# A third pair of split-weight buffers and a two-tile split lead in two windows of a diffusion backbone layer

## The chip, the core and the metric

One core of a Trainium2 chip runs the whole layer in one launch. The metric is device time in microseconds (us), lower is better. The kernel before takes 1840.38 us, the median of three runs (1839.56 to 1844.32).

## What is computed

The layer mixes 512 latent tokens of width 1024, on a grid 64 wide, with a prefix of 256 context tokens. The part that matters here, cut from the reference:

```python
hx = modulate(x, norm1_g, shift1, scale1);  hc = modulate(ctx, ...)
u_x, k_x, v_x, q_x, ga_x, gb_x = jnp.split(hx @ w_in, ...)     # 512 latent rows
u_c, k_c, v_c = jnp.split(hc @ w_in[:, :CTX_COLS], ...)        # 256 context rows
y_ssm = s5_mixer(u_x, u_c, p)               # bidirectional linear state recurrence
branch_a = s5_glu(y_ssm, p) @ w_branch_a
branch_b = na_mixer(q_x, k_x, v_x, k_c, v_c, na_rpb) @ w_branch_b
merged = sigmoid(ga_x) * branch_a + sigmoid(gb_x) * branch_b
x = x + gate1 * (merged @ w_out)
x = x + gate2 * peer_ffn(modulate(x, norm2_g, shift2, scale2), ...)
return rms_norm(x, final_g)
```

`s5_mixer` runs a scan over chunks of tokens; `peer_ffn` scores every token against all keys and experts. All is float32, and the projections are accurate beyond one reduced-precision pass.

## The kernel before

**Weight tiles.** A projection of 128 output columns is a tile of 1024 x 128 weights (some tiles have 512 rows). All tiles stand in one list, `wseq`, and are taken from it in order by `w_next` (L191): tiles 0 to 3 give u, 4 to 7 k, 8 to 11 v, 12 to 15 q, 16 to 51 are those of the two branches, the gates and the GLU, and from tile 52 on come the queries and experts of the feed-forward part. A tile is loaded by a DMA issued on SP into `wraw` (L183), rounded on ACT into `whi` (L172), and the remainder `wlo = wraw - whi` is taken on DVE (L173). TensorE then runs three passes for each of the 8 row blocks (`mm3`, L443 to L445): hi by x-hi, hi by x-lo, lo by x-hi. u, k and v tiles are also run over the context (output `mc`, against `mm` for the latent tokens).

**Buffers.** The pool `wst` has three `wraw` buffers and two each of `whi` and `wlo`. With tile i, `w_next` sees that tiles up to i+2 are loaded and that tile i+1 is split:

```python
w_ahead(i + 1, i + 1, eng)
wpos[2] += 1
w_ahead(i + 3, i + 2, eng)      # load below i+3, split below i+2
```

**Stages around the change** (times of the trace in us). Up to about 136 the outer products (`g_outer`, DVE, tile `Gc`), the kernel pieces (`k_prep`, L510 to L528: matmuls into `kk` and `yy`, a copy to `ks` on ACT at L522, stores `Kd<-ks` on SP at L526 to L528) and the first projections run together. `Gc`, `ks` and others lie in a pool `gst2` (L488), closed behind them. Then DVE sweeps the state `E` (`carry`, L610 to L613): sixteen passes of a tree, each pass two products `ta`, `tb_` and two additions into `E`; the products lie in the pool `scp` (L586). PE meanwhile projects k, v and q (L443 to L445 and, for v, transposes at L637). ACT copies the swept state to `S` (L641, L642). Attention follows from 222 to 310, one matmul chain of scores (L708, L709), softmax (DVE L710 and L712, ACT L714), transposes (L721) and values (L739), with the readout of the state. From about 310 to 460 PE runs the GLU, the branches and the gates, while DVE forms modulation vectors from streamed rows (`mod2`, L814), the gated sums (L829, L849) and the splits. Then come `wo_mm` with W_out, `x1_norm` (L922 to L931, with small tiles `ss`, `ry`, `rz` of two buffers each) and the feed-forward part.

**Order.** But for SP's first part, the order of instructions on each engine is set by a scheduler from the order of the calls; an engine then runs its list strictly in that order, and a waiting instruction holds up all behind it.

Of the kernel before, what the change touches and what calls it, by code (L numbers as in the profile page):

```python
# [10 lines left out]
F32 = mybir.dt.float32  # L11
F32R = mybir.dt.float32r
# [11 lines left out]
KD = 8  # L24
# [60 lines left out]
def tile_hybrid(ctx, tc, A, out, dbg=None):  # L85
# [3 lines left out]
    def open_pool(**kw):  # L89
        cm = tc.tile_pool(reuse_waits="tile", **kw)  # L90
        return cm, cm.__enter__()

    def close_pool(*cms):
        for cm in cms:
            cm.__exit__(None, None, None)

    def DBG(name, ap):
        if dbg is not None and name in dbg:
            sy.dma_start(dbg[name], ap)
# [9 lines left out]
    def bank(tag="mm", bufs=None):  # L109
        bufs = bufs or nb[tag]  # L110
        return (psA if tag in ("kk", "yy") else ps).tile([128, 512], F32, tag=tag, name=tag, bufs=bufs)
# [19 lines left out]
    wst = ctx.enter_context(tc.tile_pool(name="wst", bufs=1))  # L131
# [10 lines left out]
    def sm(name, *shape):  # L142
        return stp.tile([128, *shape], F32, name=name)

    wseq = [("win", m, KD) for m in range(16)]
    wkind = {"b": ("win", 24, KD), "a": ("win", 16, KD), "B": ("wb", 0, 4), "A": ("wa", 0, 4), "g": ("wglu", 0, 4)}
    for i, o in enumerate(MERGE):
        src, m0, kn = wkind[o]
# [2 lines left out]
    wseq += [("puT", j, KD) for j in range(UA)]  # L151
    wseq += [("wq", i, KD) for i in range(2 * NH)]
    wseq += [("puT", j, KD) for j in range(UA, 128)]
    mark = [None]
    wraw, wsp = {}, {}
    wext = {}
    wcnt = {}

    def wtile(kind, dt):
        n, x = wbufs[kind]  # L160
        c = wcnt[kind] = wcnt.get(kind, -1) + 1
        if wext and c % (n + x) >= n:
            return wext[0].tile([128, KD, 128], dt, tag=kind, name=kind, bufs=x)
        return wst.tile([128, KD, 128], dt, tag=kind, name=kind, bufs=n)
# [1 line left out]
    wbufs = {"wraw": (3, 2), "whi": (2, 1), "wlo": (2, 1)}  # L166
    wpos = [0, 0, 0]

    def w_split(raw, kn, eng):
        hi = wtile("whi", F32R)  # L170
        lo = wtile("wlo", F32R)
        act.copy(hi[:, :kn], raw[:, :kn])  # L172
        i = eng.tensor_sub(lo[:, :kn], raw[:, :kn], hi[:, :kn].bitcast(F32))  # L173
        if eng is gp:
            mark[0] = i.ins
        return hi, lo

    def w_ahead(load_to, split_to, eng):
        while wpos[0] < min(load_to, len(wseq)):
            i = wpos[0]  # L180
            src, m, kn = wseq[i]
            w = wtile("wraw", F32)
            sy.dma_start(w[:, :kn].rearrange("p k c -> p (k c)"), A[src][m])  # L183
            wraw[i] = w
            wpos[0] += 1
        while wpos[1] < min(split_to, len(wseq)):
            i = wpos[1]
            wsp[i] = w_split(wraw.pop(i), wseq[i][2], eng)
            wpos[1] += 1

    def w_next(want, eng=gp):  # L191
        i = wpos[2]
        assert wseq[i][:2] == want, (wseq[i], want)
        w_ahead(i + 1, i + 1, eng)
        wpos[2] += 1
        w_ahead(i + 3, i + 2, eng)
        return wsp.pop(i)

    order = tc.manual_schedule(engines={mybir.EngineType.SP})
# [15 lines left out]
    def rsqrt_mean(ss, y, z):  # L215
        dve.tensor_scalar(ss, ss, 1.0 / D, EPS, op0=ALU.mult, op1=ALU.add)
        dve.tensor_scalar(z.bitcast(I32), ss.bitcast(I32), 1, None, op0=ALU.logical_shift_right)
        dve.tensor_scalar(y.bitcast(I32), z.bitcast(I32), -1.0, 1597463007.0, op0=ALU.mult, op1=ALU.add)
        dve.tensor_scalar(ss, ss, -0.5, None, op0=ALU.mult)
        for _ in range(3):  # L220
            if y.shape[-1] == 1:
                dve.tensor_scalar(z, y, y, ss, op0=ALU.mult, op1=ALU.mult)
            else:
                dve.tensor_mul(z, y, y)
                dve.tensor_mul(z, z, ss)
            dve.scalar_tensor_tensor(y, z, 1.5, y, op0=ALU.add, op1=ALU.mult)
# [20 lines left out]
    for o in LDO:  # L247
        if o == "w":
            mod_rows(nw)
            nw += 1  # L250
        elif o == "s":
            sy.dma_start(ssm, A["ssm"][:, 0:1120])
        elif o == "p":
            sy.dma_start(colp, A["colp"])
        elif o == "r":
            sy.dma_start(crt.rearrange("p j g h -> p (j g h)"), A["ssm"][:, 1120:2144])
        elif o == "1":
            w_ahead(wpos[0] + 1, 0, gp)
        elif o == "x":
            x_t.append(load_x(A["x"], len(x_t)))  # L260
        else:
            c_t.append(load_x(A["ctx"], len(c_t)))
# [26 lines left out]
    dt, er, th = sm("dt", G), sm("er", G), sm("th", G)  # L289
# [46 lines left out]
    n = 1  # L336
# [114 lines left out]
    def project(m, ctx_too, eng=None):  # L451
        eng = eng or (dve, gp)[PJE(m)]
        w = w_next(("win", m), eng)
        a = bank()
        mm3(a, w, hxh, hxl, KD)
        if not ctx_too:
            return a, None
        c = bank("mc", 1)
        mm3(c[:, :CTXL], w, hch, hcl, KD)
        return a, c[:, :CTXL]  # L460

    w0 = w_next(("win", 0))
    wpos[2] += 1
    w1 = wsp.pop(1)
# [19 lines left out]
    ecm, ep = open_pool(name="ep", bufs=1, side="right")  # L484
# [89 lines left out]
    for o in SEQ1:  # L574
        m = nxt[o]
        nxt[o] += 1
        if o == "u":
            a, c = (a1, c1) if m == 1 else project(m, True)
# [4 lines left out]

    kcm, kp_ = open_pool(name="kp", bufs=1)

    sccm, scp = open_pool(name="scp", bufs=1, side="right")  # L586
    lam = [L8]
    for l in range(4):
# [40 lines left out]
    for m in range(4):  # L629
        a, c = project(8 + m, True)  # L630
# [3 lines left out]
        for j0, n in ((0, 4), (4, 3)):  # L634
            p = bank("tp")
# [10 lines left out]
    for m in range(4):  # L646
        a, _ = project(12 + m, False)
        av = a.rearrange("p (r j c) -> p r j c", r=8, c=16)
        for e in range(2):
            s, z = slice(64 * e, 64 * e + 64), slice(64 * (1 - e), 64 * (1 - e) + 64)  # L650
            gp.memset(qT[2 * m + e][z], 0.0)
            act.activation(qT[2 * m + e][s].rearrange("p (j r c) -> p r j c", r=8, c=16), av[s], AF.Copy, scale=0.125)
    close_pool(sccm, ecm)

    ycm, yp = open_pool(name="yp", bufs=1, side="right")
    Y = yp.tile([128, TC, SSMW // 2], F32, name="Y")
# [132 lines left out]
    for i in range(4):  # L789
        p = bank("tp")  # L790
# [8 lines left out]
        dve.tensor_sub(zl[i], zf[i], zh[i].bitcast(F32))  # L799
    DBG("zf0", zf[0])  # L800
    close_pool(ycm, xscm)

    mgcm, mgp = open_pool(name="mgp", bufs=1, side="right")
    mgh = [mgp.tile([128, SEQ], F32R, name=f"mgh{i}") for i in range(8)]
# [19 lines left out]
    def branch(which, m):  # L824
        w = w_next(("w" + which, m), dve)
        a = bank()
        xs = (ah, al) if which == "a" else (oh, ol)
        mm3(a, w, *xs, 4)
        dve.scalar_tensor_tensor(sgt[which, m], sgt[which, m], 1.0, a, op0=ALU.add, op1=ALU.mult)  # L829
# [70 lines left out]
    x1cm, x1p = open_pool(name="x1p", bufs=1)  # L900
# [22 lines left out]
    def x1_norm(t):  # L923
        sy.dma_start(x1d[t], x1[t])
        if t == 0:
            DBG("x1_0", x1[0])
        ss, y, z = (x1p.tile([128, 1], F32, tag=n, name=n, bufs=2) for n in ("ss", "ry", "rz"))
        jk = m2p.tile([128, D], BF16, tag="jk2", name="jk3", bufs=1)
        act.activation(jk, x1[t], AF.Square, accum_out=ss)
        rsqrt_mean(ss, y, z)  # L930
        act.activation(x1[t], x1[t], AF.Copy, scale=y)  # L931
# [25 lines left out]
    def wo_pass(ps_):  # L957
        for i in range(2):
            t = ps_ // 2 * 2 + i
            wo_out(ps_ % 2, t, wo_mm(ps_, t))  # L960
            if ps_ < 3:
                for k in range(4):
                    wo_load(ps_ + 1, 4 * i + k)
            if ps_ % 2:
                x1_norm(t)
# [8 lines left out]
    for half in range(2):  # L974
        p = bank("tp")
# [3 lines left out]
    DBG("hrow", hrow)  # L979
    close_pool(x1cm)  # L980
    close_pool(wocm, m2cm, mgcm)
    ugp = ctx.enter_context(tc.tile_pool(name="ugp", bufs=1))
    gate = ugp.tile([128, NT, 128], F32, name="gate")
    ijt = ugp.tile([128, 2, ND, 128], F32, name="ijt")
# [416 lines left out]
```

## Time and profile before

| | |
|---|---|
| runs (three) | 1839.56, 1840.38, 1844.32 us |
| profiled execution | 1838.56 us, of which the span of the trace is 1836.7 us |
| TensorE matmul busy | 1719.5 us (94% of the span) |
| VectorE (DVE) busy | 1471.2 us (80%) |
| ScalarE (ACT) busy | 779.4 us (42%) |
| GpSimd (POOL) busy | 354.0 us (19%) |
| mean granted TensorE clock | 0.973 |

Busy shares are means over stages that have different limits. So the windows of the changed stages are read one by one, and there the question is which engine's wait ends last. The granted clock is a share of TensorE's full clock.

### The profile page before, as it was taken

To read this page: it belongs to the slowest core of one execution; us is meant where nothing else is said; L and a number is where in the kernel's file an instruction comes from. 1 tells how busy PE (TensorE), PEld (TensorE's weight loads), DVE (VectorE), ACT (ScalarE), POOL (GpSimd) and SP (SyncE) were. 2 spreads that over 40 slices of the span, in tenths; PEclk is the share of its full clock that TensorE was granted. 3 is DMA by queue.
4 is the path that set the end of the run, shared out by engine and by line. 5 is a ranking of instruction groups with operands and counts; after the bars stand their busy time and mean duration, and the time that the engine had idled before them with its cause. 6 is when DMAs were issued, how large, how long until landed. Compare 5 with 4: busy or idle time off the path is not lost.

```text
span 1836.7 us, 27460 instructions
## 1 busy us (share of the span) xinstructions
PE 1719.5 (94%) x9941; PEld 1504.7 (82%) x9941; DVE 1471.2 (80%) x3054; ACT 779.4 (42%) x1214; POOL 354.0 (19%) x291
## 2 busy tenths in 40 slices
PE   5999899999999899995589999999999999999997
PEld 2878677778899799994579899999999999998885
DVE  8889765875699998999888788888878888884456
ACT  6452555432464346666333333333333333333332
POOL 0001000000000000000332444544545444440000
PEclk9999899999999999997699999999999999999999
DMA  8341362885544336765799899999999999994432
GB/s 334 95 134 59 95 165 58 286 292 166 201 140 140 116 117 189 207 196 170 223 406 356 273 345 348 329 342 352 318 339 359 336 327 344 341 336 128 127 119 75
DMA packets 186327, 426.15 MB, mean 232 GB/s; under 512 B 25552, under 2 KB 91216, under 8 KB 186192
## 3 DMA queue, kind: packets, MB, share of 16 engines
q1 hardware_dynamic: 84816, 231.44, 37.3%
q0 software_dynamic: 36864, 134.23, 20.2%
q10 hardware_dynamic: 64512, 58.73, 10.1%
q8 instruction: 78, 1.28, 0.3%
q14 instruction: 57, 0.47, 0.1%
HBM read 388.72 MB, written 35.62 MB: 231 GB/s over the span
## 4 chain that ended last, share of the span: by engine, by line
PE 73%; DVE 16%; DMA 5%; issue 2%; ACT 2%; SPq 0%; ACTq 0%; POOL 0%; DVEq 0%
PE acc L1273 10%; PE acc L1274 10%; PE acc L1275 10%; PE yy L445 5%; PE yy L443 5%; PE yy L444 5%; PE kk L445 5%; PE kk L443 5%; PE kk L444 5%; DVE wlo L173 3%; DMA wm<-in_wmodT_dram 3%; PE mm L443 2%; PE mm L445 2%; PE mm L444 2%; DMA Gt_d<-gs 1%
## 5 line engine op out<-in xcount | busy, mean ns | idle before, releaser
L172 ACT CAST whi<-wraw 128x1024 fp32r<-128x1024 f32 (+1 forms) x212 | 213.9, 1009 | 219.3 <-PE mm L444 100.3
L1156 POOL DMA_INDIRECT gu<-in_pu_dram,idx x128 | 167.6, 1309 | 590.1 <-ACT gs L1142 386.0
L173 DVE TENSOR_TENSOR wlo<-wraw,whi 128x1024 fp32r<-128x1024 f32 (+1 forms) x212 | 247.2, 1167 | 38.3 <-ACT whi L172 37.2
L1156 POOL DMA_INDIRECT gu<-in_pv_dram,idx x128 | 177.6, 1388 | 195.2 <-DVE gacc L1174 167.2
L1255 DVE TENSOR_TENSOR wlo<-wraw,whi 128x1024 fp32r<-128x1024 f32 x128 | 156.5, 1223 | 38.0 <-ACT whi L1254 37.7
L1163 DVE SCALAR_TENSOR_TENSOR gj<-gu,hrow 128x1024 bf16<-128x1024 f32 x128 | 156.1, 1220 | 29.6 <-DMA gu<-in_pu_dram,idx 29.2
L443 PE MATMUL yy<-hth,whi 128*128 128x384 f32 x512 | 174.7, 341 | 4.2 <-ACT whi L172 4.0
L1174 DVE SCALAR_TENSOR_TENSOR gacc<-gu,av,gacc 128x1024 f32<-128x1024 f32 x127 | 162.6, 1280 | 19.4 <-DMA gu<-in_pv_dram,idx 18.9
L445 PE MATMUL yy<-hth,wlo 128*128 128x384 f32 x512 | 174.7, 341 | 1.2 <-DVE wlo L173 1.2
L445 PE MATMUL kk<-hth,wlo 128*128 128x384 f32 x512 | 173.9, 340 | 1.4 <-DVE wlo L173 1.3
L443 PE MATMUL kk<-hth,whi 128*128 128x384 f32 x512 | 172.9, 338 | 2.4 <-ACT ring L954 2.4
L444 PE MATMUL yy<-htl,whi 128*128 128x384 f32 x512 | 174.0, 340 | 0.0
L444 PE MATMUL kk<-htl,whi 128*128 128x384 f32 x512 | 172.9, 338 | 0.0
L1254 ACT CAST whi<-wraw 128x1024 fp32r<-128x1024 f32 x128 | 133.7, 1046 | 67.7 <-PE kk L444 26.7
L1142 ACT ACTIVATE gs<-mm 128x512 f32<-128x512 f32 x96 | 94.1, 1090 | 56.1 <-PE mm L1140 53.4
L445 PE MATMUL mm<-hxh,wlo 128*128 128x512 f32 x256 | 103.8, 406 | 12.4 <-DVE wlo L173 12.4
L443 PE MATMUL mm<-hxh,whi 128*128 128x512 f32 x256 | 102.0, 403 | 4.7 <-ACT whi L172 3.0
L443 PEld LDWEIGHTS yy<-hth,whi 128*128 128x128 f32 x512 | 97.6, 191 | 7.5 <-ACT whi L172 4.7
L444 PE MATMUL mm<-hxl,whi 128*128 128x512 f32 x256 | 102.8, 402 | 0.0
L443 PEld LDWEIGHTS kk<-hth,whi 128*128 128x128 f32 x512 | 96.8, 189 | 4.5 <-ACT ring L954 2.7
L445 PEld LDWEIGHTS yy<-hth,wlo 128*128 128x128 f32 x512 | 97.3, 190 | 3.1 <-DVE wlo L173 1.7
L444 PEld LDWEIGHTS yy<-htl,whi 128*128 128x128 f32 x512 | 97.6, 191 | 2.3
(1911 smaller groups left out, 4217.4 us busy)
## 6 DMA issues: line engine op xcount, KB each, us to landing
wraw<-in_puT_dram SPq DMA_DIRECT2D x128, 512.0 KB
wraw<-in_pv_dram SPq DMA_DIRECT2D x128, 512.0 KB
Gt_d<-gs ACTq DMA_DIRECT2D x24, 1024.0 KB
gch<-Gt_d ACTq DMA_DIRECT2D x32, 768.0 KB
wraw<-in_win_dram SPq DMA_DIRECT2D x32, 512.0 KB
wm<-in_wmodT_dram SPq DMA_DIRECT2D x32, 512.0 KB
wraw<-in_wq_dram SPq DMA_DIRECT2D x32, 512.0 KB
wm<-in_wm_dram SPq DMA_DIRECT2D x16, 512.0 KB
```

The lines of the kernel that those rows point to most:

```text
L172: act.copy(hi[:, :kn], raw[:, :kn])
L173: i = eng.tensor_sub(lo[:, :kn], raw[:, :kn], hi[:, :kn].bitcast(F32))
L443: pe.matmul(o, hi[:, k], xh, start=(k == 0), stop=False)
L444: pe.matmul(o, hi[:, k], xl, start=False, stop=False)
L445: pe.matmul(o, lo[:, k], xh, start=False, stop=(k == kn - 1))
L1156: gp.indirect_dma_start(out=u, out_offset=None, in_=A[tab], in_offset=bass.IndirectOffsetOnAxis(ap=ix[:, s:s + 1], axis=0))
L1163: dve.scalar_tensor_tensor(jk, u, 1.0, hrow, op0=ALU.mult, op1=ALU.mult, accum_out=av[:, s:s + 1])
L1174: dve.scalar_tensor_tensor(gacc, u, av[:, s:s + 1], gacc, op0=ALU.mult, op1=ALU.add)
L1255: dve.tensor_sub(lo, w, hi.bitcast(F32))
L1273: pe.matmul(acc[t][half], wh_[:, ts], hi[:, cs], start=(j == 0), stop=False)
L1274: pe.matmul(acc[t][half], wh_[:, ts], lo[:, cs], start=False, stop=False)
L1275: return pe.matmul(acc[t][half], wl_[:, ts], hi[:, cs], start=False, stop=(j == 127))
```

## The change

A pool `wx` with one further `whi` and one further `wlo` buffer is opened twice, on the right side of the SBUF: from before the state sweep until q is projected, and from the GLU and branches until `wo_mm`, `x1_norm` and their pools are done. While it is open, every third tile of the string takes the `wx` pair, and loading and splitting run one tile further ahead (load below i+4, split below i+3), as far as tile 15 in the first window and tile 51 in the second. `ry` and `rz` in `x1_norm` go from two buffers to one. Line numbers after the change are higher by 6 up to L183, by 7 from there to `scp`, and by 9 to 12 behind it.

```diff
-    def wtile(kind, dt):
+    nwx = 0
+    wxp = None
+    def wtile(kind, dt, early=False):
         n, x = wbufs[kind]
+        if early and wxp is not None:
+            wcnt[kind] = c = wcnt.get(kind, -1) + 1
+            p = wxp if c % (n + 1) == n else wst
+            return p.tile([128, KD, 128], dt, tag=kind, name=kind, bufs=1 if p is wxp else n)
...
-            wsp[i] = w_split(wraw.pop(i), wseq[i][2], eng)
+            wsp[i] = w_split(wraw.pop(i), wseq[i][2], eng, i < nwx)
...
-        w_ahead(i + 3, i + 2, eng)
+        x = wxp is not None and i + 2 < nwx
+        w_ahead(i + 3 + x, i + 2 + x, eng)
...
     kcm, kp_ = open_pool(name="kp", bufs=1)
+    wxcm, wxp = open_pool(name="wx", bufs=1, side="right")
+    nwx = 16
     sccm, scp = open_pool(name="scp", bufs=1, side="right")
...
-    close_pool(sccm, ecm)
+    close_pool(sccm, wxcm, ecm)
+    wxp = None
...
     close_pool(ycm, xscm)
+    wxcm, wxp = open_pool(name="wx", bufs=1, side="right")
+    nwx = [w[0] for w in wseq].index("wq")
...
-        ss, y, z = (x1p.tile([128, 1], F32, tag=n, name=n, bufs=2) for n in ("ss", "ry", "rz"))
+        ss, y, z = (x1p.tile([128, 1], F32, tag=n, name=n, bufs=1 + (n == "ss")) for n in ("ss", "ry", "rz"))
...
     close_pool(wocm, m2cm, mgcm)
+    close_pool(wxcm)
```

**First place: PE, the last kernel pieces and tiles 5 and 6.** Tile 5 is `mm_1779` and tile 6 `mm_1842` before; after the change tile 5 is `mm_1788`. A number behind a name is the program's own. Before:

```order
L445 MATMUL mm_1779<-hxh4_94,wlo_1713 128x512
L443 MATMUL mm_1779<-hxh5_95,whi_1712 128x512
L516 MATMUL kk_1382<-Gc_1292,Bp_348 32x128 [waits DVE_49]
...
L519 MATMUL yy_1438<-crt_131,Bb_347 32x16 x8
L444 MATMUL mm_1842<-hxl1_99,whi_1775 128x512
...
L445 MATMUL mm_1842<-hxh7_97,wlo_1776 128x512
L516 MATMUL kk_1486<-Gc_1428,Bp_348 32x128 [waits DVE_49]
```

After:

```order
L523 MATMUL yy_1546<-Gc_1476,Bp_348 32x128 [waits DVE_49]
L523 MATMUL yy_1546<-Gc_1476,Bp_348 32x128
L526 MATMUL yy_1546<-crt_131,Bb_347 32x16 x8
L450 MATMUL mm_1788<-hxh0_90,whi_1717 128x512 [waits Activation_49]
L451 MATMUL mm_1788<-hxl0_98,whi_1717 128x512
```

Before, the 48 latent matmuls of tiles 5 and 6 stood between the pieces, which wait for DVE one by one; now all of them stand behind the last piece, and the first waits for ACT.

**Second place: ACT, the cast of tile 5.** `ks` are the pieces on their way to `Kd`, `kTC0` is the result of tile 4. Before, tile 5 had been cast long ago and the next cast in the list is that of tile 7:

```order
L522 COPY ks_1563<-yy_1546 32x144 x3
L561 COPY kTC0_1766<-mm_1716 128x8x8 [waits DVE_49]
...
L561 COPY kTC1_1829<-mm_1779 128x8x8
...
L561 COPY kTC2_1892<-mm_1842 128x8x8 [waits Pool_49]
...
L172 CAST whi_1838<-wraw_1773 128x1024 [waits PE_49]
```

After:

```order
L529 COPY ks_1563<-yy_1546 32x144 x3
L568 COPY kTC0_1775<-mm_1725 128x8x8 [waits DVE_49]
...
L577 COPY kTC0_1775<-mc_1750 128x256
L178 CAST whi_1717<-wraw_1054 128x1024 [waits DMAHW4_49,DMAHW3_49,DMAHW5_49,DMAHW2_49,DMAHW6_49,DMAHW1_49,DMAHW7_49,DMAHW0_49,Activation_49]
L568 COPY kTC1_1838<-mm_1788 128x8x8 [waits PE_49]
```

`whi_1717` is the first tile in `wx`, which lies where the `ks` buffers of the closed pool `gst2` lay; the semaphores it waits for are those of the stores `Kd<-ks`, to the last of them (from `ks_1503` and `ks_1563`).

**Third place: DVE, the end of the sweep.** `E_741` is the state. Before:

```order
L612 TENSOR_TENSOR E_741<-E_741,ta_1704 128x64x31 [waits DVE_49]
L173 TENSOR_TENSOR wlo_2304<-wraw_2266,whi_2303 128x1024 [waits DMAHW4_49,PE_49,Activation_49]
L613 TENSOR_TENSOR E_741<-E_741,tb__1705 128x64x31 [waits DVE_49]
L173 TENSOR_TENSOR wlo_2339<-wraw_2301,whi_2338 128x1024 [waits DMAHW5_49,PE_49,Activation_49]
L710 TENSOR_TENSOR mm_2448<-mm_2448,bs_2419 128x256 [waits DMAHW0_49,PE_49,Activation_49]
```

After:

```order
L621 TENSOR_TENSOR E_741<-E_741,ta_1707 128x64x31 [waits DVE_49]
L179 TENSOR_TENSOR wlo_2124<-wraw_2047,whi_2123 128x1024 [waits DMAHW2_49,PE_49,Activation_49]
L622 TENSOR_TENSOR E_741<-E_741,tb__1708 128x64x31 [waits DVE_49]
L179 TENSOR_TENSOR wlo_2198<-wraw_2121,whi_2197 128x1024 [waits DMAHW3_49,PE_49,Activation_49]
L179 TENSOR_TENSOR wlo_2313<-wraw_2275,whi_2312 128x1024 [waits DVE_49,DMAHW5_49,PE_49,Activation_49]
```

At the same place of the sweep DVE splits tile 14 before (`wlo_2304`) and tile 12 after (`wlo_2124`). Between the first addition into `E` and this split there stand six splits before, four after.

## Rows read from the trace of the kernel before

**Rows 1.** The chain that ended last, shares of the span by engine.

```profile
PE 73%; DVE 16%; DMA 5%; issue 2%; ACT 2%; SPq 0%; ACTq 0%; POOL 0%; DVEq 0%
```

**Rows 2.** Stages: stretch, length, busy us of PE, PEld, DVE, ACT, POOL; PEclk, DMA.

```profile
118.00:133.00 15.00, 15.00 (x163) 11.01 (x164) 12.44 (x36) 3.80 (x12) 0.00 (x0) 1.00 0.59 171
...
195.00:210.00 15.00, 8.25 (x28) 6.34 (x29) 14.97 (x9) 3.20 (x5) 0.00 (x0) 0.77 0.12 36
...
222.00:310.00 88.00, 87.74 (x736) 67.28 (x735) 51.74 (x115) 46.39 (x128) 0.00 (x0) 1.00 0.45 117
310.00:412.00 102.00, 96.16 (x439) 76.31 (x437) 81.25 (x127) 45.42 (x67) 0.00 (x0) 1.00 0.83 271
412.00:460.00 48.00, 46.43 (x202) 38.30 (x203) 25.17 (x39) 13.61 (x20) 0.00 (x0) 0.96 0.52 165
```

**Rows 3.** What PE waited for from 118 to 225: total, times, longest.

```profile
PE mm L445 <- DVE wlo L173: 7.4, 2, 5.3
PE mc L443 <- ACT kTC L570: 2.9, 1, 2.9
PE mm L443 <- ACT whi L172: 1.0, 1, 1.0
```

**Rows 4.** Timeline of PE: start, us, instruction, idle before.

```profile
136.21 0.38 PE L443 MATMUL mc<-hc,whi 128*128 128x256 f32 x1 [2.90 <-ACT kTC L570]
...
152.82 0.40 PE L445 MATMUL mm<-hxh,wlo 128*128 128x512 f32 x1
...
157.37 0.39 PE L444 MATMUL mm<-hxl,whi 128*128 128x512 f32 x1
157.59 0.28 PE L443 MATMUL mc<-hc,whi 128*128 128x256 f32 x1
...
158.31 0.28 PE L443 MATMUL mc<-hc,whi 128*128 128x256 f32 x1
...
199.69 0.80 PE L445 MATMUL mm<-hxh,wlo 128*128 128x512 f32 x1 [5.35 <-DVE wlo L173]
200.29 0.63 PE L443 MATMUL mm<-hxh,whi 128*128 128x512 f32 x1
...
202.85 0.59 PE L443 MATMUL mm<-hxh,whi 128*128 128x512 f32 x1
...
222.27 0.59 PE L708 MATMUL mm<-kTC,q 128*128 128x256 f32 x2
...
223.47 0.66 PE L721 MATMUL tp<-ident,P 128*128 128x128 f32 x4 [0.18 <-ACT P L714]
```

**Rows 5.** Timeline of DVE around the state sweep.

```profile
131.45 0.42 DVE L333 TENSOR_TENSOR Gc<-Gc,ga 128x256 f32<-128x256 f32 x1
...
138.01 1.23 DVE L610 TENSOR_TENSOR ta<-E,L 128x1024 f32<-128x1024 f32 x1 [5.83 <-DMA Kd<-ks]
140.74 1.23 DVE L611 TENSOR_TENSOR tb__1615<-E,L 128x1024 f32<-128x1024 f32 x1 [1.50 <-DMA Kd<-ks]
...
143.30 1.22 DVE L612 TENSOR_TENSOR E<-E,ta 128x1024 f32<-128x1024 f32 x1
...
207.90 1.22 DVE L173 TENSOR_TENSOR wlo<-wraw,whi 128x1024 fp32r<-128x1024 f32 x1
```

**Rows 6.** The costliest groups: the weight casts.

```profile
L172 ACT CAST whi<-wraw 128x1024 fp32r<-128x1024 f32 (+1 forms) x212 | 213.9, 1009 | 219.3 <-PE mm L444 100.3
```

**Rows 7.** Timeline of SP's DMA queue: the last store of the kernel pieces.

```profile
139.12 0.42 SPq L528 DMA_DIRECT2D Kd<-ks  x1
```

**Rows 8.** What PE waited for from 310 to 460.

```profile
PE mm L445 <- DVE wlo L173: 5.6, 7, 2.8
PE mm L443 <- DVE sg L829: 1.7, 1, 1.7
```

**Rows 9.** What ACT waited for from 310 to 460.

```profile
ACT whi L172 <- PE mm L444: 50.9, 21, 9.5
```

**Rows 10.** Timeline of ACT in x1_norm.

```profile
513.25 1.15 ACT L931 ACTIVATE x<-x,ry 128x1024 f32<-128x1024 f32 x1 [1.07 <-DVE ry L226]
```

More of the change, by code (lines that the diff above doesn't have):

```diff
@@ L167, in tile_hybrid, with w_split @@
     wpos = [0, 0, 0]
-    def w_split(raw, kn, eng):
-        hi = wtile("whi", F32R)
-        lo = wtile("wlo", F32R)
+    def w_split(raw, kn, eng, early=False):
+        hi = wtile("whi", F32R, early)
+        lo = wtile("wlo", F32R, early)
         act.copy(hi[:, :kn], raw[:, :kn])
```

## The prediction, made before the changed kernel ran

> **What bounds the kernel now.** I read the chain that ended last, then busy time by stage, then what PE waits for inside the stages that the change touches, then the instructions around the longest waits. The chain is PE for 73% and DVE for 16% [rows 1], so a change in the supply of weights counts only where PE stands still. The stages differ. From 118 to 133 PE is busy all 15.00 us, from 195 to 210 only 8.25 of 15.00, and its granted clock there is 0.77; in attention, 222 to 310, it is busy 87.74 of 88 us [rows 2]. So a shift that enters attention passes through it whole, with nothing to absorb it. From 310 to 412 PE misses 5.84 us and from 412 to 460 another 1.57, together 7.4 [rows 2].
>
> The waits for splits are the target. Around the state sweep PE waits twice for a `wlo`, 7.4 us in all and 5.3 the longest, and once 1.0 for a `whi` [rows 3]. In the branches it waits seven times for a `wlo`, 5.6 us, and once 1.7 for `sg`, which no weight buffer helps [rows 8]. There the casts are released by PE's matmuls, 50.9 us of waiting in 21 times [rows 9]: the cast stands ready and waits for a free `whi`. That is what a third buffer cures. Around the sweep the reader should look elsewhere: at 138.01 and 140.74 the sweep's first two products wait for the stores `Kd<-ks` to land [rows 5], the last of them issued at 139.12 [rows 7]. Before that moment the memory of `ks` isn't free, and by the order shown above `wx` lies on it.
>
> **First window: what moves.** Tile 5 is the first in `wx`. Its cast waits for the last `Kd` stores, and PE's list has all latent matmuls of tiles 5 and 6 behind it. One latent matmul takes (157.37 - 152.82) / 20 = 0.2275 us, 24 of them 5.46; one context matmul (158.31 - 157.59) / 6 = 0.12, 24 of them 2.88 [rows 4]. So 48 x 0.2275 = 10.9 us of work that filled PE between 118 and 133, in gaps between kernel pieces that wait for DVE, go behind the stores. PE can do nothing in their place: the pieces keep their pace, set by DVE's outer products, which end at 131.45 + 0.42 = 131.9 [rows 5].
>
> When does PE go on? The stores land at 140.74 before. Without tile 6's last 18 matmuls ahead of the last pieces this can come 18 x 0.2275 = 4.1 earlier, or not at all: 136.6 to 140.7. I take 138.0, where the first half of these stores was down before. The cast adds 1.0 [rows 6], so PE goes on at 139.0.
>
> Before, PE ran from 136.21 to 222.27 [rows 4], 86.1 us: 9 latent tiles x 5.46 = 49.1, 7 context tiles x 2.88 = 20.2, waits 7.4 + 1.0 = 8.4, and a rest of 8.4 (transposes, the first scores, slower matmuls after the stalls). After, 11 latent tiles are due, 60.1 us, with the same 20.2.
>
> The stall is the open term. At the sweep's end DVE reaches its split 207.90 - 143.30 = 64.6 us after the first addition into `E` [rows 5]. Afterwards that addition comes one cast and one split of 1.2 (the row of 207.90) after the stores, at 140.2, and two splits fewer stand between, so this split begins at 140.2 + 64.6 - 2.4 = 202.4 and ends at 203.6. But it is tile 12's now, not tile 14's. PE reaches it after 7 latent tiles (38.2), 6 context tiles (17.3) and about half of the rest (4): 139.0 + 59.5 = 198.5. It stalls for 5.1, about as long as the 5.35 now. One stall instead of two also saves a slow restart: after the one of 199.69 six matmuls took 202.85 - 200.29 = 2.56, against 6 x 0.2275 = 1.37, so some 1.4 with the seventh [rows 4]. The end of q: 139.0 + 60.1 + 20.2 + 7.0 + 5.1 = 231.4, against 222.27, **+9.1**.
>
> Then the first softmax. Now its transposes come 1.20 after the last projection (223.47) [rows 4], since the first scores stood among the last tile's matmuls; after the change four splits stand on DVE ahead of the first score's addition. No row prices this; it lies between nothing and two splits, 2.4, and as PE has state readout to do meanwhile, I take +1. First window: **+10**. Low end: no stall, no slow restart, stores at 136.6, ramp 0: 10.1 - 5.1 - 1.4 - 1.4 - 1 = +1.2. High end: stores at 140.7 and a ramp of 2.4: +14.2.
>
> **Second window.** The GLU and branches take a third pair, and `ks` is long gone. The seven waits of 5.6 are the gain; the first two fall within the first tiles, before a lead can form, and I leave 1.1 of them: **-4.5**. Ends: 0, if the splits are late for DVE's own queue (it is busy 81.25 of 102 us [rows 2]), and -7.4, if all idle time goes.
>
> **`ry` and `rz`.** With one buffer each, a norm can't start its short chain on DVE until ACT has read the last `ry`; ACT's scaling takes 1.15 us and waits 1.07 for `ry` as it is [rows 10]. Between 0 and 1.2; **+0.4**, since the statistics on ACT overlap. Everything behind keeps its length, and what the merge gains is carried to the end because the norms wait for PE's output.
>
> **Sum.** 10.1 - 4.5 + 0.4 = +6.0 on the profiled execution of 1838.56, 1844.6. That execution lies 1.8 below the median of the runs, 1840.38, so I forecast the median at 1846.4.
>
> **Rivals.**
>
> *The buffers do what they are for in both windows* (the other side). Then the sweep's waits (8.4) and the branches' (5.6) go, 14.0 us: 1826.4. For it: casts that wait for a free `whi` in 21 places [rows 9]. Against it: the first cast in `wx` waits for `Kd`'s stores, and 10.9 us of PE work wait with it. It decides by one point: is `wx` free before PE has done tile 4, near 118? The waits are unequal, 5.3 of 7.4 in one and 2.8 of 5.6 in another, not one gap at each tile. [...] Chance 0.08.
>
> *The stall at tile 12 is gone.* If the sweep ends some 5 us earlier than I work out, the first window costs 10.1 - 5.1 - 1.4 = 3.6, and the sum is -0.5: 1839.9. For it: DVE is free of the early wait once the stores land. Against it: sixteen passes at their old price and four splits lie between. Chance 0.22, with 0.02 of it below -5.5.
>
> *Later and nothing back.* The stores land as now, 140.7 (+2.7), and DVE's queue keeps the branches' waits: 10.1 + 2.7 + 0.4 = +13.2, 1853.6. Chance 0.12.
>
> That the change does nothing is excluded by the order rows: it moves 48 matmuls.
>
> **How the numbers follow.** My forecast has 0.58. A measurement here tells 0.3%, 5.5 us, from no change. Within my forecast the unknown ends spread the sum from about +1 to +11, so 0.20 of it lies within 5.5 us and 0.38 above. Slower: 0.38 + 0.12 = 0.50. The same: 0.20 + 0.20 = 0.40. Faster: 0.08 + 0.02 = 0.10. The range runs from 1837.5, which takes in most of the second rival, to 1853.6, the third; below it lies the first, and some 0.15 in all is left out.
>
> **What would show it.** Right: PE idle or at kernel pieces only, from about 119 to 139; the cast of tile 5 released by the stores `Kd<-ks`, at 137 to 141; one wait of 4 to 6 us for a `wlo` near 200; the first scores near 231; attention as long as before; the `wlo` waits from 310 on down from 5.6 to about 1. Wrong: projection matmuls between 119 and 133, or the cast of tile 5 before 133; no stall near 200; the branches' waits as before or grown. If attention begins near 231 and the end still isn't later by about 6, the second window gave back more than its idle time, and my view of what bounds that stage is wrong.

## The result, and the profile after

The changed kernel takes 1858.04 us, the median of five runs (1854.61 to 1862.96), against 1842.3 for five runs of the kernel before (1839.56 to 1846.47). The ratio is 1.0085 (95% interval 1.0066 to 1.0105): some 16 us slower, where 6 were forecast, and outside the range. The profiled execution took 1860.02, with a span of 1858.0.

The stages of the changed kernel, with the columns of [rows 2]:

```profile
118.00:133.00 15.00, 6.79 (x127) 4.14 (x125) 13.41 (x38) 5.27 (x17) 0.00 (x0) 0.68 0.51 151
133.00:142.00 9.00, 1.82 (x29) 1.47 (x30) 3.97 (x10) 3.11 (x9) 0.92 (x10) 0.50 0.27 79
142.00:195.00 53.00, 53.00 (x285) 45.92 (x284) 52.28 (x80) 11.40 (x28) 4.40 (x10) 0.95 0.16 50
195.00:210.00 15.00, 11.19 (x57) 9.37 (x56) 14.54 (x8) 3.64 (x6) 0.25 (x2) 0.85 0.11 35
222.00:310.00 88.00, 87.48 (x682) 66.84 (x681) 48.50 (x101) 44.90 (x116) 0.00 (x0) 1.00 0.48 130
310.00:412.00 102.00, 97.64 (x488) 77.93 (x487) 74.98 (x124) 47.83 (x81) 0.00 (x0) 0.98 0.68 221
412.00:460.00 48.00, 44.70 (x188) 35.99 (x188) 31.99 (x52) 11.87 (x18) 0.00 (x0) 0.96 0.67 220
```

From 118 to 133 PE is busy 6.79 us instead of 15.00, and its granted clock is 0.68 there and 0.50 from 133 to 142. In attention it is as full as before. From 310 to 460 it is idle for 4.36 + 3.30 = 7.7 us, against 7.4 before; the stage's boundaries have moved by 16, so this is a rough comparison, and the waits below make it exact.

PE around the sweep, in the timeline (start, us, instruction, idle before), to be held against [rows 4]:

```profile
133.85 0.40 PE L526 MATMUL yy<-crt,Bb 128*32 128x16 f32 x8
...
141.42 0.79 PE L450 MATMUL mm<-hxh,whi 128*128 128x512 f32 x1 [7.18 <-ACT whi L178]
...
142.87 0.63 PE L450 MATMUL mm<-hxh,whi 128*128 128x512 f32 x1
...
147.13 0.54 PE L451 MATMUL mm<-hxl,whi 128*128 128x512 f32 x1
...
206.39 0.79 PE L452 MATMUL mm<-hxh,wlo 128*128 128x512 f32 x1 [3.81 <-DVE wlo L179]
...
235.03 0.59 PE L718 MATMUL mm<-kTC,q 128*128 128x256 f32 x2
...
240.51 0.66 PE L731 MATMUL tp<-ident,P 128*128 128x128 f32 x4 [0.52 <-ACT P L724]
```

The last kernel piece is done at 133.85 + 0.40; then PE waits 7.18 us for the cast of tile 5. From 142.87 to 147.13 ten matmuls take 4.26 us, 0.426 each, at a granted clock of 0.50; at 1.00, in the kernel before from 152.82 to 157.37, it is 0.2275 [rows 4]. One long wait for a split is left, 3.81 us. The first scores come at 235.03 instead of 216.37 and the first transposes of attention at 240.51 instead of 223.47. For comparison, PE's last wait for a split and the first scores in the kernel before:

```profile
209.17 0.50 PE L445 MATMUL mm<-hxh,wlo 128*128 128x512 f32 x1 [2.06 <-DVE wlo L173]
...
216.37 0.59 PE L708 MATMUL mm<-kTC,q 128*128 128x256 f32 x2
```

In both kernels this last wait ends with the split at the end of the sweep. Before, 46 latent matmuls of q stand behind it in PE's list (counted in the trace); after the change there are 94, the 48 of two tiles more, and 24 for the context. So q ends late although the split comes 2.8 us earlier, at 206.39 instead of 209.17.

ACT, in the timeline: the cast of tile 5, and in the branches the activation `ah` of the GLU.

```profile
140.33 1.04 ACT L178 CAST whi<-wraw 128x1024 fp32r<-128x1024 f32 x1 [3.83 <-DMA Kd<-ks]
...
367.48 0.63 ACT L862 ACTIVATE ah<-sg 128x512 fp32r<-128x512 f32 x1 [6.35 <-DVE sg L861]
```

The cast is released by the stores `Kd<-ks`, as the order said. The second row belongs to the branches: ACT does nothing for 6.35 us, while casts stand behind.

DVE, in the timeline, at the beginning and the end of the sweep and in the branches:

```profile
137.61 1.23 DVE L620 TENSOR_TENSOR tb__1618<-E,L 128x1024 f32<-128x1024 f32 x1
...
142.55 1.22 DVE L621 TENSOR_TENSOR E<-E,ta 128x1024 f32<-128x1024 f32 x1
...
205.12 1.22 DVE L179 TENSOR_TENSOR wlo<-wraw,whi 128x1024 fp32r<-128x1024 f32 x1
...
365.61 1.22 DVE L826 SCALAR_TENSOR_TENSOR jk<-wm,cb 128x1024 bf16<-128x1024 f32 x1 [2.24 <-DMA wm<-in_wmodT_dram]
```

The sweep's second product, at 140.74 before [rows 5], now starts at 137.61. From the first addition into `E` (142.55) to the split for which PE waits (205.12) DVE has hardly a gap: from 142 to 195 it is busy 52.28 of 53.00 us. So DVE sets the end of PE's wait, and a PE that came there earlier would only wait longer. The last row is a modulation product that waits for its row to land; `sg`, for which `ah` waits, stands behind it.

What PE waited for in the branches of the changed kernel (326 to 481: total, times, longest), to be held against [rows 8]:

```profile
PE mm L450 <- ACT whi L178: 3.2, 1, 3.2
PE mm L452 <- DVE wlo L179: 2.9, 1, 2.9
PE mm L450 <- ACT ah L862: 1.2, 1, 1.2
```

Seven short waits for splits are gone. In their place come one for a cast, one for a split and one for `ah`, 7.3 us (and 0.5 for `sg`), about what stood there before.

**Where the time went.** The starts of first and last instructions on PE in the two profiles give the lengths of five stages. The pieces end at 132.9 before and 133.8 after. From there to the last transposes of attention it is 173.5 and 188.7 us, to the first matmul with W_out 155.6 and 157.1, to the first accumulation of the expert stage 470.9 and 472.7, and to the last 891.0 and 892.9. So 15.2 of 21.3 us lie in the first window, and the second gave nothing back. (These two executions lie 3.7 below and 2.0 above the medians of their kernels; that is why they differ by more than 16.)

### The profile page after: what moved, and what is told of

It reads as the page before. It is cut to its first block, busy times and chain, and to the rows that moved or that the text cites. A ratio compares the mean times of both kernels' runs of the same rounds, so it can differ in the third digit from the quotient of the medians.

```text
span 1858.0 us, 27472 instructions
## 1 busy us (share of the span) xinstructions
PE 1729.2 (93%) x9941; PEld 1513.0 (81%) x9941; DVE 1471.3 (79%) x3054; ACT 779.2 (42%) x1214; POOL 347.9 (19%) x291
## 4 chain that ended last, share of the span: by engine, by line
PE 75%; DVE 16%; DMA 5%; issue 2%; ACT 1%; SPq 0%; POOL 0%; DVEq 0%; ACTq 0%; POOLq 0%
PE acc L1286 10%; PE acc L1287 9%; PE acc L1288 9%; PE kk L452 5%; PE kk L450 5%; PE yy L450 5%; PE yy L452 5%; PE kk L451 5%; PE yy L451 5%; PE mm L450 3%; PE mm L452 3%; PE mm L451 3%; DVE wlo L179 2%; DMA wm<-in_wmodT_dram 2%; PE tp L731 1%
## 5 line engine op out<-in xcount | busy, mean ns | idle before, releaser
L1169 POOL DMA_INDIRECT gu<-in_pv_dram,idx x128 | 174.9, 1367 | 198.7 <-DVE gacc L1187 170.0
L1267 ACT CAST whi<-wraw 128x1024 fp32r<-128x1024 f32 x128 | 133.8, 1047 | 64.1 <-PE kk L451 24.0
L450 PE MATMUL mm<-hxh,whi 128*128 128x512 f32 x256 | 104.5, 413 | 12.8 <-ACT whi L178 12.3
L452 PEld LDWEIGHTS kk<-hth,wlo 128*128 128x128 f32 x512 | 97.2, 190 | 7.5 <-DVE wlo L179 6.5
L451 PEld LDWEIGHTS kk<-htl,whi 128*128 128x128 f32 x512 | 97.2, 190 | 1.7
```

What stands on the lines that cost most here:

```text
L450: pe.matmul(o, hi[:, k], xh, start=(k == 0), stop=False)
L451: pe.matmul(o, hi[:, k], xl, start=False, stop=False)
L452: pe.matmul(o, lo[:, k], xh, start=False, stop=(k == kn - 1))
L1169: gp.indirect_dma_start(out=u, out_offset=None, in_=A[tab], in_offset=bass.IndirectOffsetOnAxis(ap=ix[:, s:s + 1], axis=0))
```

## The experiments

The first theory after the result: the loss is made ahead of the sweep, because `wx` lies where `ks` lay, so that 10.9 us of PE work wait with tile 5's cast and PE restarts at the lower granted clock (0.50 from 133 to 142). Its rivals: the second window costs as well, or the longer lead itself does harm. The lengths of the stages in every profile (us, from the starts of PE's instructions as above; each stage runs from the end of the one to its left):

| run | pieces end | attention | branches | to experts | experts | median of all runs |
|---|---|---|---|---|---|---|
| before | 132.9 | 173.5 | 155.6 | 470.9 | 891.0 | 1842.3 |
| after | 133.8 | 188.7 | 157.1 | 472.7 | 892.9 | 1858.04 |
| first_only | 134.2 | 187.2 | 155.6 | 469.8 | 894.5 | 1856.67 |
| second_only | 134.8 | 174.8 | 159.5 | 467.6 | 892.1 | 1844.33 |
| first_late | 134.2 | 178.6 | 157.8 | 469.2 | 896.0 | 1846.85 |
| first_above | 132.8 | 186.1 | 158.6 | 468.5 | 897.6 | 1856.7 |
| first_free | 136.7 | 174.1 | 161.4 | 469.6 | 900.2 | 1851.25 |
| before_u1 | 135.7 | 175.2 | 156.9 | 473.0 | 891.3 | 1849.73 |
| first_fill | 136.1 | 183.1 | 159.0 | 472.6 | 893.8 | 1853.52 |
| before_nowm | 135.4 | 174.0 | 148.8 | 479.0 | 894.5 | 1846.27 |
| second_nowm | 133.9 | 174.9 | 147.5 | 473.7 | 895.0 | 1838.49 |
| before_nowait | 132.8 | 174.8 | 154.5 | 474.0 | 895.9 | 1845.72 |
| wm4 | 134.4 | 174.1 | 146.8 | 477.5 | 896.6 | 1844.97 |
| wm3 | 133.1 | 174.0 | 150.5 | 472.5 | 892.1 | 1840.36 |

One execution stands behind each row, the medians have five to twelve. The ratios below are against runs of the kernel before taken beside each run, with medians from 1842.0 to 1843.6. The columns *to experts* and *experts* vary by 11 and 9 us although their code is, but for `ry`, `rz` and the number of `wm2` buffers, the same in all. Each of these edits makes the scheduler order the later stages differently than before; these columns show how much of a total is that. The other columns aren't free of it: *branches* runs from 155.6 to 161.4 in the seven kernels whose edit doesn't touch that stage, and *attention* from 173.5 to 174.9 in the seven whose edit lies behind it. A difference within these spreads shows nothing by itself.

One count sorts the column *attention*: the latent matmuls that PE runs from 108 to its last kernel piece. They are 72 in the kernel before, first_late, first_free and before_u1, whose columns are 173.5 to 178.6. They are 24, the same 48 fewer each time, in the changed kernel, first_only, first_above and first_fill, whose columns are 183.1 to 188.7.

**The first window alone.**

```diff
-    wxcm, wxp = open_pool(name="wx", bufs=1, side="right")
-    nwx = [w[0] for w in wseq].index("wq")
...
-    close_pool(wxcm)
```

> The first window alone (sweep to q), ry and rz with two buffers as before. Theory 1, the loss is made before the sweep (tile 5's cast waits until the stores of ks have landed, since wx lies on ks, and 10.9 us of PE work wait with it at a clock that has fallen): the whole loss stays, +14 to +18 us against the kernel before, attention 16 later, everything behind it shifted by that and no more. Rival, the second window costs as well: only +10 to +13 here, and the rest in the run of the second window alone.

Ratio 1.0081 (1.0066 to 1.0096), +15 us. All but 1 us of the loss is here, mostly in the attention column, 187.2 against 173.5.

**The second window alone.** The first opening, its `nwx = 16` and its closing are taken out.

> The second window alone (branches to the last norm), with ry and rz of one buffer. Theory 1: no gain and no loss, -3 to +2 us against the kernel before, since the small waits for splits are replaced by others behind the modulation rows on DVE. My own forecast of this part was -4.5 + 0.4 = -4.1. Rival, the second window costs as well: +3 to +6.

Ratio 1.0019 (1.0007 to 1.0030), +3.5 us: not a gain, and the forecast of -4.1 falls; so does the theory's range, and the result lies in the rival's. Its waits of PE in the branches:

```profile
PE mm L450 <- ACT whi L178: 4.0, 1, 4.0
PE mm L452 <- DVE wlo L179: 3.8, 2, 3.4
```

They are waits of the same two kinds as in the changed kernel. The branches take 159.5 us, which lies within the spread of kernels whose branches weren't touched, so it isn't shown that the third pair by itself makes this stage longer; shown is that it doesn't make it shorter. With the first window's 15 the parts make 18.5; both together make 16, within the intervals.

**Lead from tile 7 on.** Tiles 5 and 6 keep the old pairs.

```diff
+    nwx, wx0 = 0, 7
-            p = wxp if c % (n + 1) == n else wst
+            p = wxp if (c - wx0) % (n + 1) == 0 else wst
...
-        x = wxp is not None and i + 2 < nwx
+        x = wxp is not None and wx0 <= i + 1 and i + 2 < nwx
```

> The first window alone, but lead and wx begin with tile 7: tiles 5 and 6 keep the two old pairs and stand among the kernel pieces on PE as before; tile 7 is the first in wx, and its cast waits for the stores of ks. Theory 1: the loss is gone, -6 to +3 us against the kernel before, PE busy from 118 to 133. Rival, the longer lead itself does the harm (more casts and splits ahead in ACT's and DVE's order around the sweep): +5 or more remain.

Ratio 1.0034 (1.0021 to 1.0048), +6 us. PE is busy all 15.00 us from 118 to 133 again and 9 us of the loss are gone, but not all: what remains is in the rival's range. Now the cast of tile 7 is late for PE (the profile puts its release, at 141.82, down to PE, so that the stores alone hold it isn't shown), and the waits go on to the softmax:

```profile
143.86 0.79 PE L450 MATMUL mm<-hxh,whi 128*128 128x512 f32 x1 [1.96 <-ACT whi L178]
...
212.82 0.79 PE L452 MATMUL mm<-hxh,wlo 128*128 128x512 f32 x1 [3.39 <-DVE wlo L179]
...
230.65 0.66 PE L731 MATMUL tp<-ident,P 128*128 128x128 f32 x4 [1.50 <-ACT P L724]
```

**The pools in the other order.** `scp` is opened ahead of `wx`, so the sweep's products lie on `ks` as before.

> The first window alone with the two pools opened in the other order, so that the products of the sweep lie on ks as before, and wx lies elsewhere: tile 5's cast then waits for the last stores of Gc instead of those of ks. PE's order around tile 5 stays as in the changed kernel (all pieces first, then tiles 5 and 6). Theory 1: the cast comes some 6 us earlier (near 134), the sweep starts 3 later as before, and the loss falls to +5 to +11 us. Rival, the moved order alone sets the loss, not the memory: +14 to +18 as in the first window alone.

Ratio 1.0083 (1.0067 to 1.0099), +15: the rival was right. PE in the timeline:

```profile
136.44 0.80 PE L450 MATMUL mm<-hxh,whi 128*128 128x512 f32 x1 [3.23 <-ACT whi L178]
...
190.47 0.50 PE L452 MATMUL mm<-hxh,wlo 128*128 128x512 f32 x1 [1.81 <-DVE wlo L179]
...
205.55 0.79 PE L452 MATMUL mm<-hxh,wlo 128*128 128x512 f32 x1 [4.04 <-DVE wlo L179]
```

The cast came early enough for PE to restart at 136.44, 5 us sooner than in the first window alone (141.47), but the attention column is only 1.1 shorter. The wait for tile 12's split ends at 205.55, against 206.58 there: the sweep on DVE sets it, so what PE gains ahead it waits for there. So it isn't the wait for the stores that costs; it is that the 10.9 us of tiles 5 and 6 are behind the pieces at all. What put them there was, as we read the orders, that the first cast depends on memory of `gst2` at all: here, by the order of the pools, on the stores of `Gc`. In the next kernel, where it doesn't, the 48 matmuls stand among the pieces again.

**`wx` in memory that was free all along,** with its control. One `uT` buffer is given up, and `wx` is opened ahead of `gst2`; the lead starts at tile 5 as in the change. The control is the kernel before with one `uT` buffer.

```diff
-        uT = gst2.tile([128, TC, NCK], F32, tag="uT", name="uT", bufs=2)
+        uT = gst2.tile([128, TC, NCK], F32, tag="uT", name="uT", bufs=1)
```

> The first window alone with wx in memory that was free all along: one of the two uT buffers is given up and wx opened ahead of gst2, with the same lead from tile 5 on. Tile 5's cast waits for nothing, and tiles 5 and 6 stand among the kernel pieces again, while the sweep can start 3 earlier as in the changed kernel. Theory 1 (where wx lies makes the loss): -6 to +2 us against the kernel before, PE busy from 118 to 133. Rival (the longer lead itself harms the sweep, as the +5 to +6 of the run that began with tile 7 suggests): +3 to +8.

> The kernel before with one uT buffer instead of two, the control of the run with wx in free memory (+8 us). Theory 1: the single buffer costs 2 to 4 us near 98 and the reordering of later stages some more, so +3 to +8 here, and the first window in free memory costs nothing by itself. Rival: the single buffer costs nothing (within 2), and the longer lead costs +6 to +8.

Ratios 1.0044 (1.0029 to 1.0060) and 1.0043 (1.0027 to 1.0058). The single `uT` buffer costs 8 us in all, the window nothing on top. The stretch from 118 to 133 of the first of the two, and its waits of PE:

```profile
118.00:133.00 15.00, 14.29 (x140) 10.80 (x128) 12.87 (x37) 5.11 (x17) 0.00 (x0) 1.00 0.48 141
```

```profile
207.31 0.80 PE L452 MATMUL mm<-hxh,wlo 128*128 128x512 f32 x1 [5.15 <-DVE wlo L179]
...
226.60 1.02 PE L718 MATMUL mm<-kTC,q 128*128 128x256 f32 x2 [4.05 <-ACT q L661]
```

PE is nearly full among the pieces, and the attention column, 174.1 against 175.2, gains at most 1.1 from the third buffer; as its pieces end 1.0 later, the last transposes of attention come at the same time in both (310.8 and 310.9). So the lead is worth little in this window even with its memory free: the split behind the sweep is still 5.15 us late, and q's copies on ACT, 4.05.

**Matmuls whose result nobody reads,** 82 of them, in the first window's kernel.

```diff
+        if m == 1:
+            fp = bank("tp")
+            for j in range(82):
+                pe.matmul(fp, hxh[j % KD][:, 0:128], hxh[(j + 1) % KD], start=True, stop=True)
```

> The first window alone, as in its first run, with 82 additional matmuls whose result nobody reads, placed where PE waits between the kernel pieces and ahead of tile 5. If the clock that fell while PE stood idle is part of the loss: granted clock near 1.00 from 118 to 150 and 4 to 6 us faster than the first window alone, +9 to +11 against the kernel before. If the clock is not part of it: +14 to +18 as without them.

Ratio 1.0055 (1.0040 to 1.0069), against 1.0081 without. The stretches 118 to 133 and 133 to 142, first without them, then with:

```profile
118.00:133.00 15.00, 7.00 (x126) 4.32 (x124) 13.30 (x38) 5.14 (x17) 0.00 (x0) 0.70 0.51 151
133.00:142.00 9.00, 1.79 (x29) 1.48 (x30) 4.25 (x11) 3.24 (x10) 0.92 (x10) 0.50 0.27 79
```

```profile
118.00:133.00 15.00, 15.00 (x134) 11.29 (x136) 13.74 (x39) 5.25 (x16) 0.00 (x0) 1.00 0.43 129
133.00:142.00 9.00, 9.00 (x92) 6.78 (x81) 3.14 (x8) 3.75 (x13) 0.92 (x10) 1.00 0.44 117
```

The granted clock is 1.00 in place of 0.70 and 0.50. From the first to the 24th latent matmul after PE's restart it is 8.35 us in the changed kernel, 6.95 in the first window alone and 5.59 with the additional matmuls; the granted clock from 142 to 195 is 0.95, 0.98 and 1.00 on average. So the lower clock takes 2.8 and 1.4 us of PE's time there.

By the expectation the 10 us against the kernel before say that the clock is part of the loss. The trace doesn't bear it out. DVE's sweep and PE's wait for its last split, first without the additional matmuls:

```profile
142.59 1.22 DVE L621 TENSOR_TENSOR E<-E,ta 128x1024 f32<-128x1024 f32 x1
...
205.31 1.22 DVE L179 TENSOR_TENSOR wlo<-wraw,whi 128x1024 fp32r<-128x1024 f32 x1
206.44 2.22 DVE L622 TENSOR_TENSOR E<-E,tb__1708 128x1984 f32<-128x1984 f32 x1
206.58 0.80 PE L452 MATMUL mm<-hxh,wlo 128*128 128x512 f32 x1 [5.36 <-DVE wlo L179]
```

Then with them:

```profile
143.63 1.22 DVE L626 TENSOR_TENSOR E<-E,ta 128x1024 f32<-128x1024 f32 x1
...
204.05 1.22 DVE L180 TENSOR_TENSOR wlo<-wraw,whi 128x1024 fp32r<-128x1024 f32 x1
205.19 2.22 DVE L626 TENSOR_TENSOR E<-E,ta 128x1984 f32<-128x1984 f32 x1
205.33 0.80 PE L453 MATMUL mm<-hxh,wlo 128*128 128x512 f32 x1 [4.58 <-DVE wlo L180]
207.44 2.23 DVE L627 TENSOR_TENSOR E<-E,tb__1708 128x1984 f32<-128x1984 f32 x1
```

PE waits for DVE in both, 5.36 and 4.58 us, so time that it saves ahead of this wait is lost in it. The wait ends 1.25 us earlier, although the sweep starts 1.0 later, because the split stands one addition into `E` (2.22 us) further ahead in DVE's list, and not because of the clock. The first scores come 1.4 earlier. The rest of the fall of the column, from 187.2 to 183.1, is mostly that the pieces end 2.0 later. What makes the median faster isn't shown: the profiled execution, the slowest of its six, is longer than the one without (spans of 1857.4 and 1854.1). So the clock fell and slowed some matmuls, but that it makes a share of the loss isn't shown.

**The branches without the modulation loads.** The loop `mod2` loads one row block and uses it 32 times, in the kernel before and with the second window.

> The kernel before, whose modulation loop in the branches loads one row block once and uses it 32 times, so that 31 of the 32 loads are left out and the second norm's modulation is computed from other rows. If these loads hold the branches by way of DVE's queue: 3 to 8 us faster than the kernel before, waits of PE for splits down to 2 at most from 310 to 460. If they do not: within 2.

> The second window alone with the same 31 loads left out. Theory 1 (casts and splits stand behind instructions that wait for these loads, so a third buffer cannot help): without them the two kernels differ by less than 2 us, and the new waits of 3 to 4 us for a cast and a split are gone. Rival (the longer lead does harm by itself in this window): still 3 or more slower than the kernel before with the same loads left out. My forecast's view (the third buffer helps): 3 to 5 faster than that kernel.

Ratios 1.0012 (1.0001 to 1.0023) and 0.9971 (0.9961 to 0.9982). In the branches both do what the theory says: 148.8 and 147.5 us, PE's waits there down to one of 1.7 in the second:

```profile
PE mm L450 <- ACT whi L178: 1.7, 1, 1.7
```

So with the loads out of the way the two branches differ by 1.3, which is within what the order alone moves. The totals miss both expectations: the first kernel was to be 3 to 8 us faster than the kernel before, and the two were to differ by less than 2. The kernel before gains 6.8 there and is yet 2 slower: its next stage takes 479.0 instead of 470.9. The difference of the two totals, 7.8 us, is mostly that stage, and not a gain of the third pair.

**The loads kept, but nobody waits for them.** DVE's product reads the conditioning row instead.

> The kernel before with all 32 loads of modulation rows kept, but DVE's products read the conditioning row in their place, so that nothing waits for a load; the second norm's modulation is wrong in value. If waiting in DVE's queue is what the loads cost: branches (last attention transpose to first matmul with W_out, 155.5 us before) about 149, as without the loads. If their traffic is: still 153 to 156.

Ratio 1.0022 (1.0008 to 1.0035), branches 154.5. By the expectation, this speaks for traffic. The waits show something else: PE waits 4.73 us once, for a cast, and ACT 4.9 for that cast's weights:

```profile
358.05 0.80 PE L443 MATMUL mm<-hxh,whi 128*128 128x512 f32 x1 [4.73 <-ACT whi L172]
```

```profile
ACT whi L172 <- DMA wraw<-in_win_dram: 4.9, 1, 4.9
```

So in this run PE waits for a weight load that came late. The run doesn't separate waiting from traffic; the next does.

**The 8 KB spent on modulation rows.** `wm2` has four buffers, `wx` isn't there; then three, with `ry` and `rz` as before.

```diff
-        w = m2p.tile([128, D], F32, tag="wm2", name="wm2", bufs=2)
+        w = m2p.tile([128, D], F32, tag="wm2", name="wm2", bufs=4)
```

> The kernel before, with the 8 KB that the change gives to a third pair of split buffers spent on two more buffers for the modulation rows (four instead of two), ry and rz of one buffer. Theory 1 (in the branches DVE's queue waits for these rows to land, one after the other): the branches get 3 to 6 shorter, and the kernel 2 to 6 faster than before. Rival (the loads' traffic is the limit, not their lead): branches within 2 of before.

> The kernel before with three buffers for the modulation rows, and ry and rz left with two, the candidate for a version that beats both. Theory (the branches wait for these rows, but what they give up is lost again between W_out and the expert stage, whose order the edit also changes): branches 148 to 152 against 155.6, the kernel within 0.3% of before. Rival (the loss behind the branches was peculiar to the run with four buffers): 4 to 7 us faster than before.

With four, the same loads and no third pair, the branches take 146.8, 8.8 us less than before, and DVE's waits for modulation rows, 16.4 us in 20 times in the kernel before, are down to one. First before, then with four buffers:

```profile
DVE jk L814 <- DMA wm<-in_wmodT_dram: 16.4, 20, 1.8
```

```profile
DVE jk L814 <- DMA wm<-in_wmodT_dram: 0.2, 1, 0.2
```

So the lead of these loads bounded the branches, not their traffic and not the split buffers; both kernels lie well below the spread of 155.6 to 161.4. Yet the kernel takes 1.0014 (1.0001 to 1.0028) of before, where 2 to 6 us less were expected: 6.6 are lost again on the way to the experts and 5.6 in them. With three the branches take 150.5 and the kernel 0.9984 (0.9972 to 0.9996), 3 us faster than before, as the theory expected, against 4 to 7 by the rival; it is the fastest kernel of this study that leaves nothing out. The gain in the branches is 5.1, and 2.6 of it are lost behind them.

## Why the prediction was wrong

In the profiles the two windows miss by about as much: attention ends 16.1 us later where 10.1 were forecast, and the branches are 1.5 longer where 4.5 were to be gained.

**Right: the mechanism of the first window.** Tile 5's cast is released by the stores of `ks`, PE does only the pieces from 120 to 134, one wait of 3.8 for a split stands at 206, attention is as long as before, and everything is shifted through it. 10.9 of the 15.2 us are the moved matmuls, which now stand behind the split at the end of the sweep, and PE's waits from the last piece on are the same sum before and after (2.9 + 7.4 + 1.0 = 11.3 by [rows 3], and 7.2 + 3.8 + 0.5 = 11.5): the lead won back nothing of them.

**Mis-sized: the end of q.** The forecast was "139.0 + 60.1 + 20.2 + 7.0 + 5.1 = 231.4"; the first score behind q came at 235.0, 3.6 later. Of this, 2.8 is the end of the stall: 206.39 instead of 203.6. The stores landed at about 140.3 instead of 138.0, near the upper end (140.7) of what I had allowed, and so PE restarted at 141.42 and the first addition into `E` came at 142.55 instead of 140.2. The sweep's length was right, 62.6 us to the split against 62.2. What stands behind the split took 28.6 us, where the terms of the sum leave 27.8, +0.8. I also took the PE that idles among the pieces for a PE that takes 0.2275 us a matmul, though my row for a slow restart (2.56 us for six) was there [rows 4]. The lower clock (0.50) took 2.8 us from PE at its restart, but ahead of the stall, which was 3.8 instead of 5.1; it didn't move the end of q.

**Mis-sized: the ramp into attention.** I took +1, and no more than 2.4. At the first transposes of attention it is 17.0 - 12.8 = 4.3: q ended 12.8 later, these transposes 17.0 later. Attention itself takes 0.9 less, so 3.3 are left at its last transposes, 16.1 later.

**Wrong: the second window.** "The seven waits of 5.6 are the gain" is the step that failed. [Rows 9] showed casts that wait for a free buffer, and I read this as what binds. It bound the casts, but PE waited for something else in the end. DVE's products wait for modulation rows, `sg` stands behind them in DVE's list, `ah` on ACT behind `sg`, and casts behind `ah`. A third buffer changes which of them waits. The runs show +3.5 alone, and that two more buffers for the modulation rows take 8.8 us off the same stage. These waits of DVE (16.4 us) stand in the trace of the kernel before. My low end of 0 and the rival *later and nothing back* allowed for them as "DVE's queue", but I gave that rival 0.12. Both of its conditions came true, stores that land near 140.7 and waits in the branches as before, and its 1853.6 is the nearest of the forecasts to the measured 1858.04. Whether the +3.5 is the third pair or the order that goes with it stays open.

**Wrong by omission: the stages behind.** I wrote "Everything behind keeps its length". It varies by some 10 us from one order to the next, so a shift of 5 in a stage can't be carried to the end as it is. In the changed kernel this added little (1.8 + 1.9 in the profiles); in the runs with shorter branches it took most of the gain.

`ry` and `rz` with one buffer made DVE wait for ACT, 1.0 us in two times from 470 to 560, a wait that the kernel before doesn't have:

```profile
DVE ry L225 <- ACT x L943: 1.0, 2, 0.8
```

PE's waits from 455 to 560 were 0.9 us before and are 1.3 after, and none of them names `ry`. The rival in which the buffers do their work in both windows is refuted for the first window even with memory free: at most 1.1 us of gain against waits of 8.4. The sweep's waits were unequal already before, 5.3 of 7.4 us in one [rows 3], and a further split buffer didn't close them: with its memory free one of 5.15 is left. In the branches memory did close them, but for another stream: with one more buffer for the modulation rows (wm3) PE's waits for a `wlo` from 310 to 460 are 1.2 us in one time, against 5.6 in seven [rows 8].

**Left open.** What keeps 5 us in the attention column when the lead begins with tile 7 (178.6 against 173.5), and what makes the kernel with additional matmuls faster, isn't shown. Why the stage between W_out and the experts grows when the branches get shorter (479.0 and 477.5 in two of the three shortest) isn't settled; only that its order differs from kernel to kernel. Nor was tile 5 tried among the pieces with `wx` on `ks`, since that would take a wait away that the shared memory needs.

## What to carry to other kernels

Before you add a buffer, look at what lies in its memory until when, and what work the engine's list puts behind the first tile that must wait for it; here the tile that waited dragged along 48 matmuls, 10.9 us, that the scheduler had used to fill gaps. Where casts wait for a free buffer, follow the wait one engine further: if their results would only queue behind a list that waits for another stream, give the memory to that stream. Before you price a gap or slow matmuls on PE, look for its next wait for another engine: if it waits there anyway, what counts is when that engine is done and how much of PE's work is left behind it.

## What the runs showed of the hardware that I had not expected

With only small pieces to do between its waits, PE was granted a clock of 0.68 on average from 118 to 133 and, while it waited 7.18 us for the cast, 0.50 from 133 to 142. Ten of the next large matmuls then took 0.426 us each, at 0.50, instead of 0.2275 at 1.00. Matmuls of no use in the same gaps kept the clock at 1.00 from 118 to 142. Still, in the two profiles the time won at the restart went into a later wait for DVE, of 4.58 us with these matmuls.
